# Two-layer trunk on one core: the feed-forward's first block with seven products for three chunk pairs, and other PSUM banks for the down blocks

## The chip, the core and the metric

The kernel runs on one core of one Trainium2 chip. The metric is the device time of one execution, in microseconds (us); the figure for a kernel is the median of its runs. The core has five engines with instruction queues of their own, which meet through semaphores: TensorE (matrix products, shown as PE, its weight loads as PEld), VectorE (DVE), ScalarE (ACT), GpSimd (POOL) and SyncE (SP, which here issues the loads of weights). Matrix products accumulate in eight PSUM banks of 128 x 512 float32 each, numbered 0 to 7.

## What is computed

Two layers over 256 tokens of width 2048, in float32. Each layer is a mixer (layer 0: sparse attention and gated linear attention; layer 1: stick-breaking attention), a feed-forward and a gated embedding, each with a normalisation ahead and a residual behind. The change lies in the feed-forward:

```python
def _swiglu(h, norm_g, w_gate, w_up, w_down):
    xn = _rmsnorm(h, norm_g)
    return (jax.nn.silu(xn @ w_gate) * (xn @ w_up)) @ w_down

for i in range(DEPTH):                      # DEPTH = 2
    h = h + mixer_i(h)
    h = h + _swiglu(h, ffn_norm[i], ffn_w_gate[i], ffn_w_up[i], ffn_w_down[i])
    gate = jax.nn.sigmoid(_rmsnorm(h, ple_norm[i]) @ ple_w_gate[i])
    h = h + (p[i] @ ple_w_proj[i]) * gate
```

The hidden width is 5632, which makes 11 blocks of 512 columns in each feed-forward.

## The kernel before

**Precision.** Every float32 operand of a product is split in two parts: ScalarE casts the high part (line 106) and VectorE subtracts it from the value to get the low part (line 107). A product is then three matmuls: high by high, high by low, low by high. Activations are split once; weights are split as they stream in.

**Units and tiles.** A `unit` loads four chunks of 128 weight rows (1 MB, one DMA of SP) into a raw tile; there are three raw tiles in turn inside the feed-forward. It splits two chunks at a time into a pair of tiles `whi` and `wlo`, of which there are four in turn, and with each pair of tiles issues 12 matmuls: two chunks by two halves of 128 tokens by three. A `block` is the units over all chunks of one set of 512 columns; its two banks (one for each half of the tokens) come in turn from banks 0 and 1 or 2 and 3 (`mm_tile`), unless the caller names them. Work that belongs to other steps, such as the turns of the next operand (`turn_h`), waits in a queue (`later`) and is taken out one entry for each pair of chunks (`tick`), or at once where it is needed (`need`). The order on each engine is not that of the source: a scheduler places an instruction earlier where its operands are ready earlier.

**The feed-forward.** The 11 blocks go in groups of three, three, three and two. For each block, gate and up columns are computed, then silu(gate) times up is turned across partitions (`cross`, line 143 and DMAs) and split into the hidden operand (`split_hid`). While the blocks of a group are computed, the four down blocks of the group before are placed behind them: one behind each of the first two blocks of a group, two behind the third, or two behind each block of the last group. A down block adds its two banks to the residual h (`add_to_h`, line 268). The down blocks of the last group come at the end.

**Seven products.** Blocks 1 to 10 (`gate_up_7`) do the first 6 of the 16 chunks in three chunk pairs. For a chunk pair, two halves of the tokens, gate and up, the plain way has 8 products; here there are 7, of sums of the operands. The sums of the operand (`sums_of_operand`, lines 837 to 845, into `ST`) are made once in a feed-forward; the sums of the weights (lines 858, 861, 862, into `T`) for each pair. A pair is four pieces of 6, 6, 6 and 3 matmuls (line 849), with banks as below. The other 10 chunks are classical units: after each of the first two pairs one of gate, after the third pair the last half unit of gate and then all of up. The combinations of the banks are put together by a ScalarE copy and VectorE adds into `E` (lines 898 to 907). Block 0 (`gate_up_8`) is two classical blocks; its products go straight to silu and to the product with up.

```python
    B2, B4, B3, B22, B1, B5, B6, B7 = range(8)
            pieces = [(None, raw[:, :, 0], [(B1, tok(0, 0)), (B2, tok(1, 0))]),
                      (sums_13, T[:, 0:2], [(B5, comb(0)), (B7, comb(2))]),
                      (sums_24, T[:, 2:4], [(B6, comb(1)), (B4, tok(1, 1))]),
                      (None, raw[:, 1, 1:2], [(B3, comb(3))])]
```

So bank 0 is B2, bank 1 is B4, bank 2 is B3, bank 3 is B22, bank 4 is B1, and banks 5, 6 and 7 are B5, B6 and B7.

Of the kernel before, what the change touches and what calls it, by code (L numbers as in the profile page):

```python
# [9 lines left out]
F32 = mybir.dt.float32  # L10
F32R = mybir.dt.float32r
I32 = mybir.dt.int32
AF = mybir.ActivationFunctionType
# [3 lines left out]
P = 128  # L17
NT = 2
# [9 lines left out]
def trunk_kernel(ctx: ExitStack, tc: tile.TileContext, x, p, even_norm, even_w_in, even_w_gk,  # L28
# [179 lines left out]

    def unit(ps, stat, k0, cols, first, last, nk=KU, kw0=None, step=KU, pre=None, begun=0):

# [11 lines left out]
        for j in range(0, nk, 2):  # L222
# [5 lines left out]
            for c in range(2):  # L228
                k = k0 + j + c
                for tt in range(NT):  # L230
                    sh = stat[0][:, k, tt * P:(tt + 1) * P]
                    sl = stat[1][:, k, tt * P:(tt + 1) * P]
                    st = first and tt >= begun and j + c == 0
                    en = last and j + c == nk - 1
                    nc.tensor.matmul(ps[tt][:, :n], sh, hi[:, c, :n], start=st, stop=False)  # L235
                    nc.tensor.matmul(ps[tt][:, :n], sh, lo[:, c, :n], start=False, stop=False)  # L236
                    nc.tensor.matmul(ps[tt][:, :n], sl, hi[:, c, :n], start=False, stop=en)  # L237
# [589 lines left out]
    def ffn(i, xs, nkey, nx_fn, fp):  # L827
# [22 lines left out]

        def pair(j, b):

# [21 lines left out]
            for n, (made, src, ps) in enumerate(pieces):  # L874
# [5 lines left out]
                for c, (p, stat) in enumerate(ps):  # L880
                    product(p, stat, hi[:, c], lo[:, c], j == 0, j == NS - 1 and p >= B1)
                if n % 2:
                    tick()

        def gate_up_7(b):
            need(("sT", i))
            rest = [(n, k) for n in range(2) for k in range(2 * NS, KC, KU)]

            def classical(n, k):
                nk = min(KU, KC - k)  # L890
                unit([bank[:, 2 * n], bank[:, 2 * n + 1]], xs, k, [((ffn_w_gate[i], ffn_w_up[i])[n], b * NB, NB)],
                     n == 1 and k == 2 * NS, k + nk == KC, nk=nk, begun=1)

            for j in range(NS):
                pair(j, b)
                if j < NS - 1:
                    classical(*rest.pop(0))
# [16 lines left out]

        def gate_up_8(b):
            pg = block(xs, [(ffn_w_gate[i], b * NB, NB)], key=nkey)
            rs = rstd_of(nkey)
            sl = fp.tile([P, NT, NB], F32, name="sl", bufs=1)
            for tt in range(NT):
                nc.scalar.activation(sl[:, tt], pg[tt], AF.Silu, scale=rs[:, tt:tt + 1])  # L920
            later(sums_of_operand, key=("sT", i))
            return sl, block(xs, [(ffn_w_up[i], b * NB, NB)])

        def split_hid(dst, x, k0):
# [4 lines left out]

        def gate_up(gi, n):  # L930
            b = groups[gi][n]
            if n == 0:
                hT[gi] = (fp.tile([P, 12, NT * P], F32R, name="hH"), fp.tile([P, 12, NT * P], F32R, name="hL"))
            sl, pu = gate_up_7(b) if b else gate_up_8(b)
            rs = rstd_of(nkey)
# [6 lines left out]

        def down(gi, cb, nx):
            for b in groups[gi]:
                need(("hT", i, b))
            nk = 4 * len(groups[gi])
            ps = block(hT[gi], [(ffn_w_down[i], cb * NB, NB)], nk=nk, kw=groups[gi][0] * 4)
            add_to_h(ps, cb)
            if nx:
                finish_cols(nx, cb)  # L950

        third["pool"] = fp
        for gi, g in enumerate(groups):
            for n in range(len(g)):
                gate_up(gi, n)
                if gi:
                    for cb in range(4 * n // len(g), 4 * (n + 1) // len(g)):
                        down(gi - 1, cb, None)
        nx = nx_fn()
# [161 lines left out]
```

## Time and profile before

| | us |
|---|---|
| median of 3 runs | 2417.17 (2416.87 to 2420.09) |
| the profiled execution | 2414.99 |
| its span, first to last instruction | 2413.3 |
| TensorE busy in it | 2385.1 |
| VectorE busy in it | 1722.3 |
| ScalarE busy in it | 1269.2 |

The span is what the profile shows of an execution; the difference to the execution's own time lies before and after it. The mean granted clock of TensorE is 0.999 of full speed. Times in the rows are from the span's start. A matmul's time overlaps that of its neighbours, so the cost of one is read from start to start. "idle before" is the time that an engine stood still ahead of an instruction, with what ended it; a group of instructions is named by line, engine, operation and output<-input tile. The feed-forward of layer 0 begins at about 388.9 us, that of layer 1 at about 1591.5 us.

### The profile page before, as it was taken

The numbers are of one execution on the slowest core, as the hardware profiler recorded it, in microseconds if no ns is written. First come the engines' busy times: TensorE is split into PE (matmuls) and PEld (weight loads), VectorE is DVE, ScalarE is ACT, GpSimd is POOL, SyncE is SP. The second block draws the span as 40 slices with busy tenths as digits, with TensorE's granted clock in tenths as the row PEclk, the third lists the DMA queues.
The fourth block names the chain that finished last, engine by engine and source line by source line (L and its number), as shares of the span: only waits on it lengthen the run. The fifth ranks groups of instructions, "written<-read, shape, count | busy, mean of one in ns | idle before, by whom it ended". The sixth has DMA issues, their size and how long they took to land.

```text
span 2413.3 us, 28118 instructions
## 1 busy us (share of the span) xinstructions
PE 2385.1 (99%) x10786; PEld 1959.9 (81%) x10786; DVE 1722.3 (71%) x2009; ACT 1269.2 (53%) x1560; POOL 105.3 (4%) x177
## 2 busy tenths in 40 slices
PE   8999999999999999999999999999999999999998
PEld 7887788788888888888888888887888888888887
DVE  5765456898878877855666666568988778777564
ACT  6644445555545545546546655555655455445463
POOL 0000100010000000000000000000000000000000
PEclk9999999999999999999999999999999999999999
DMA  6454455566666666555554454556666666666563
GB/s 213 141 178 140 157 207 182 194 228 215 218 221 210 212 224 226 196 197 183 175 192 157 157 178 166 203 186 199 234 213 214 212 210 212 221 231 204 178 235 122
DMA packets 240681, 473.13 MB, mean 196 GB/s; under 512 B 12849, under 2 KB 19729, under 8 KB 240418
## 3 DMA queue, kind: packets, MB, share of 16 engines
q1 hardware_dynamic: 232514, 447.07, 55.8%
q0 software_dynamic: 7744, 23.08, 3.1%
q8 instruction: 84, 1.38, 0.2%
q10 hardware_dynamic: 288, 1.18, 0.1%
q14 instruction: 51, 0.42, 0.0%
HBM read 457.66 MB, written 13.63 MB: 195 GB/s over the span
## 4 chain that ended last, share of the span: by engine, by line
PE 79%; DVE 9%; DMA 6%; ACT 3%; issue 2%; SPq 0%; DVEq 0%; ACTq 0%; POOLq 0%; POOL 0%
PE bank L236 22%; PE bank L237 22%; PE bank L235 22%; PE bank L849 9%; DVE wlo L107 4%; DMA raw<-in_ffn_w_up_dram 3%; DMA raw<-in_odd_w_in_dram 2%; DVE kT L135 1%; ACT whi L106 1%; PE bank L165 1%; DVE work L858 1%; DVE work L907 1%; DVE tq L143 0%; DVE sl L937 0%; DMA raw<-in_even_w_in_dram 0%
## 5 line engine op out<-in xcount | busy, mean ns | idle before, releaser
L107 DVE TENSOR_TENSOR wlo<-raw,whi 128x1024 fp32r<-128x1024 f32 (+2 forms) x848 | 982.8, 1172 | 474.6 <-ACT whi L106 470.3
L106 ACT CAST whi<-raw 128x1024 fp32r<-128x1024 f32 (+2 forms) x848 | 851.6, 1011 | 839.6 <-PE bank L237 561.7
L236 PE MATMUL bank<-wlo,aH 128*128 128x512 f32 (+2 forms) x2176 | 844.4, 388 | 6.8 <-DVE wlo L107 6.0
L235 PE MATMUL bank<-whi,aH 128*128 128x512 f32 (+2 forms) x2176 | 849.3, 391 | 0.6 <-ACT whi L106 0.6
L237 PE MATMUL bank<-whi,aL 128*128 128x512 f32 (+2 forms) x2176 | 842.4, 387 | 0.0
L236 PEld LDWEIGHTS bank<-wlo,aH 128*128 128x128 f32 x2176 | 409.3, 188 | 96.2 <-DVE wlo L107 16.2
L235 PEld LDWEIGHTS bank<-whi,aH 128*128 128x128 f32 x2176 | 409.1, 188 | 84.2 <-issue 2.8
L237 PEld LDWEIGHTS bank<-whi,aL 128*128 128x128 f32 x2176 | 409.0, 188 | 83.9 <-issue 1.0
L235 PE MATMUL bank<-whi,hH 128*128 128x512 f32 x704 | 277.2, 394 | 0.0
L236 PE MATMUL bank<-wlo,hH 128*128 128x512 f32 x704 | 277.0, 393 | 0.0
L237 PE MATMUL bank<-whi,hL 128*128 128x512 f32 x704 | 273.6, 389 | 0.0
L106 ACT CAST whi<-work 128x1024 fp32r<-128x1024 f32 x120 | 126.0, 1050 | 159.6 <-PE bank L237 81.9
L107 DVE TENSOR_TENSOR wlo<-work,whi 128x1024 fp32r<-128x1024 f32 x120 | 146.6, 1222 | 57.1 <-ACT whi L106 56.3
L849 PE MATMUL bank<-whi,sT 128*128 128x512 f32 x480 | 167.4, 389 | 0.0
L235 PEld LDWEIGHTS bank<-whi,hH 128*128 128x128 f32 x704 | 132.2, 188 | 30.0
L237 PEld LDWEIGHTS bank<-whi,hL 128*128 128x128 f32 x704 | 132.1, 188 | 29.7
L236 PEld LDWEIGHTS bank<-wlo,hH 128*128 128x128 f32 x704 | 132.4, 188 | 26.1
L849 PEld LDWEIGHTS bank<-whi,sT 128*128 128x128 f32 x480 | 90.1, 188 | 18.6
L147 POOL DMA_DIRECT2D ty<-tq x88 | 48.5, 560 | 1095.5 <-DVE tq L143 987.3
L849 PE MATMUL bank<-wlo,sT 128*128 128x512 f32 x240 | 94.0, 392 | 0.5 <-DVE wlo L107 0.4
L858 DVE TENSOR_TENSOR work<-raw 128x1024 f32<-128x1024 f32 x60 | 73.4, 1223 | 25.5 <-DMA raw<-in_ffn_w_up_dram 25.1
L849 PE MATMUL bank<-whi,aH 128*128 128x512 f32 x180 | 70.7, 393 | 4.3 <-DVE h L268 4.3
(253 smaller groups left out, 1620.0 us busy)
## 6 DMA issues: line engine op xcount, KB each, us to landing
raw<-in_ffn_w_down_dram SPq DMA_DIRECT2D x88, 1024.0 KB, 5.2
raw<-in_ffn_w_gate_dram SPq DMA_DIRECT2D x48, 1024.0 KB, 5.2
raw<-in_ffn_w_up_dram SPq DMA_DIRECT2D x48, 1024.0 KB, 5.2
raw<-in_odd_w_in_dram SPq DMA_DIRECT2D x48, 1024.0 KB, 5.2
raw<-in_ffn_w_gate_dram SPq DMA_DIRECT2D x80, 512.0 KB, 3.9
raw<-in_ffn_w_up_dram SPq DMA_DIRECT2D x80, 512.0 KB, 4.8
raw<-in_even_w_in_dram SPq DMA_DIRECT2D x36, 1024.0 KB, 5.0
raw<-in_ple_w_gate_dram SPq DMA_DIRECT2D x28, 1024.0 KB, 5.1
```

Source lines behind the costliest of these rows:

```text
L106: state["cast"] = nc.scalar.copy(hi, raw).ins
L107: nc.vector.tensor_tensor(lo, raw, hi.bitcast(F32), OP.subtract)
L135: nc.vector.transpose(dst[32 * a:32 * a + 32, :, :, 32 * q:32 * q + 32], src.rearrange("p t (m a c) -> p t m a c", a=4, c=32)[32 * q:32 * ...
L147: nc.gpsimd.dma_start(y[:, :, q].rearrange("a c t n -> c a (t n)"), tq[32 * q:32 * q + 32].rearrange("c a t m r -> c a (t m r)"))
L165: nc.tensor.transpose(ps[:, c, tt, :], h[:, tt, k * P:(k + 1) * P], ident)
L235: nc.tensor.matmul(ps[tt][:, :n], sh, hi[:, c, :n], start=st, stop=False)
L236: nc.tensor.matmul(ps[tt][:, :n], sh, lo[:, c, :n], start=False, stop=False)
L237: nc.tensor.matmul(ps[tt][:, :n], sl, hi[:, c, :n], start=False, stop=en)
L849: nc.tensor.matmul(bank[:, p], a, b, start=first and m == 0, stop=last and m == 2)
L858: nc.vector.tensor_tensor(T[:, 0:2], raw[:, 0], raw[:, :, 1], OP.add)
L907: nc.vector.tensor_tensor(e, bank[:, 2 * n:2 * n + 2], e, OP.add)
```

## The change

Block 0 of each feed-forward now goes the same way as the others, with one difference in order. Two classical units (chunks 6 to 9 of gate, then of up) come first; then all turns of the operand and its sums are asked for; then come the three pairs with a classical unit after each of the first two (chunks 10 to 13 of gate, then of up), and last the half units (chunks 14 and 15) of gate and of up. A set `begun` notes which banks have been started. `gate_up_8` is gone. The queue entry for `sums_of_operand` is made ahead of the two units and may be taken at once. The down blocks that stand between blocks get their banks by name: the last one behind a block banks 1 and 6 (B4, B6), one before it banks 0 and 5 (B2, B5). The last group's down blocks take turns on banks 0 to 3 as before.

```diff
--- before.py
+++ after.py
@@ -206,7 +206,7 @@
             return third["pool"].tile([P, KU, NB], F32, name="raw3", bufs=1)
         return wp.tile([P, KU, NB], F32, name="raw", bufs=2)
 
-    def unit(ps, stat, k0, cols, first, last, nk=KU, kw0=None, step=KU, pre=None, begun=0):
+    def unit(ps, stat, k0, cols, first, last, nk=KU, kw0=None, step=KU, pre=None, starts=None):
 
 
         kw0 = k0 if kw0 is None else kw0
@@ -230,7 +230,7 @@
                 for tt in range(NT):
                     sh = stat[0][:, k, tt * P:(tt + 1) * P]
                     sl = stat[1][:, k, tt * P:(tt + 1) * P]
-                    st = first and tt >= begun and j + c == 0
+                    st = (first if starts is None else starts[tt]) and j + c == 0
                     en = last and j + c == nk - 1
                     nc.tensor.matmul(ps[tt][:, :n], sh, hi[:, c, :n], start=st, stop=False)
                     nc.tensor.matmul(ps[tt][:, :n], sh, lo[:, c, :n], start=False, stop=False)
@@ -848,7 +848,7 @@
             for m, (a, b) in enumerate(((stat[0], hi), (stat[0], lo), (stat[1], hi))):
                 nc.tensor.matmul(bank[:, p], a, b, start=first and m == 0, stop=last and m == 2)
 
-        def pair(j, b):
+        def pair(j, b, begun):
 
             raw = raw_tile().rearrange("p (r c) n -> p r c n", r=2)
             for c, w in enumerate((ffn_w_gate[i], ffn_w_up[i])):
@@ -878,21 +878,35 @@
                 lo = wp.tile([P, 2, NB], F32R, name="wlo")
                 split_sb(src, hi[:, :len(ps)], lo[:, :len(ps)])
                 for c, (p, stat) in enumerate(ps):
-                    product(p, stat, hi[:, c], lo[:, c], j == 0, j == NS - 1 and p >= B1)
+                    product(p, stat, hi[:, c], lo[:, c], p not in begun, j == NS - 1 and p >= B1)
+                    begun.add(p)
                 if n % 2:
                     tick()
 
-        def gate_up_7(b):
-            need(("sT", i))
+        def gate_up(b):
+            begun = set()
             rest = [(n, k) for n in range(2) for k in range(2 * NS, KC, KU)]
 
             def classical(n, k):
                 nk = min(KU, KC - k)
-                unit([bank[:, 2 * n], bank[:, 2 * n + 1]], xs, k, [((ffn_w_gate[i], ffn_w_up[i])[n], b * NB, NB)],
-                     n == 1 and k == 2 * NS, k + nk == KC, nk=nk, begun=1)
-
+                ps = (2 * n, 2 * n + 1)
+                for c in range(k // 2, (k + nk) // 2):
+                    need((nkey, c))
+                unit([bank[:, p] for p in ps], xs, k, [((ffn_w_gate[i], ffn_w_up[i])[n], b * NB, NB)],
+                     False, k + nk == KC, nk=nk, starts=[p not in begun for p in ps])
+                begun.update(ps)
+
+            if b == 0:
+
+                later(sums_of_operand, key=("sT", i), delay=0)
+                rest.sort(key=lambda u: u[1])
+                classical(*rest.pop(0))
+                classical(*rest.pop(0))
+                for c in range(KC // 2):
+                    need((nkey, c))
+                need(("sT", i))
             for j in range(NS):
-                pair(j, b)
+                pair(j, b, begun)
                 if j < NS - 1:
                     classical(*rest.pop(0))
             nc.scalar.copy(E[:, 0], bank[:, B1])
@@ -912,26 +926,17 @@
             turns["mm"] = 0
             return sl, [E[:, 2 + tt] for tt in range(NT)]
 
-        def gate_up_8(b):
-            pg = block(xs, [(ffn_w_gate[i], b * NB, NB)], key=nkey)
-            rs = rstd_of(nkey)
-            sl = fp.tile([P, NT, NB], F32, name="sl", bufs=1)
-            for tt in range(NT):
-                nc.scalar.activation(sl[:, tt], pg[tt], AF.Silu, scale=rs[:, tt:tt + 1])
-            later(sums_of_operand, key=("sT", i))
-            return sl, block(xs, [(ffn_w_up[i], b * NB, NB)])
-
         def split_hid(dst, x, k0):
             d = [dst[n][:, k0:k0 + 4, :].rearrange("p m (q r) -> p m q r", q=8) for n in range(2)]
             with tc.issue_after(state["cast"]):
                 nc.scalar.copy(d[0], x)
             nc.vector.tensor_tensor(d[1], x, d[0].bitcast(F32), OP.subtract)
 
-        def gate_up(gi, n):
+        def hidden(gi, n):
             b = groups[gi][n]
             if n == 0:
                 hT[gi] = (fp.tile([P, 12, NT * P], F32R, name="hH"), fp.tile([P, 12, NT * P], F32R, name="hL"))
-            sl, pu = gate_up_7(b) if b else gate_up_8(b)
+            sl, pu = gate_up(b)
             rs = rstd_of(nkey)
             for tt in range(NT):
                 nc.vector.scalar_tensor_tensor(sl[:, tt], pu[tt], rs[:, tt:tt + 1], sl[:, tt], op0=OP.mult,
@@ -940,11 +945,11 @@
             later(lambda: x.update(x=cross(sl, fp)), key=("xT", i, b))
             later(lambda: split_hid(hT[gi], x["x"], 4 * n), key=("hT", i, b), after=(("xT", i, b), 10))
 
-        def down(gi, cb, nx):
+        def down(gi, cb, nx, ps=None):
             for b in groups[gi]:
                 need(("hT", i, b))
             nk = 4 * len(groups[gi])
-            ps = block(hT[gi], [(ffn_w_down[i], cb * NB, NB)], nk=nk, kw=groups[gi][0] * 4)
+            ps = block(hT[gi], [(ffn_w_down[i], cb * NB, NB)], nk=nk, kw=groups[gi][0] * 4, ps=ps)
             add_to_h(ps, cb)
             if nx:
                 finish_cols(nx, cb)
@@ -952,10 +957,13 @@
         third["pool"] = fp
         for gi, g in enumerate(groups):
             for n in range(len(g)):
-                gate_up(gi, n)
+                hidden(gi, n)
                 if gi:
-                    for cb in range(4 * n // len(g), 4 * (n + 1) // len(g)):
-                        down(gi - 1, cb, None)
+                    cbs = range(4 * n // len(g), 4 * (n + 1) // len(g))
+                    for cb in cbs:
+
+                        ps = (B4, B6) if cb == cbs[-1] else (B2, B5)
+                        down(gi - 1, cb, None, [bank[:, p] for p in ps])
         nx = nx_fn()
         for cb in range(4):
             down(len(groups) - 1, cb, nx)
```

## Rows read from the trace of the kernel before

**Rows 1.** The page's first part: each engine's busy time, share and instructions.

```profile
PE 2385.1 (99%) x10786; PEld 1959.9 (81%) x10786; DVE 1722.3 (71%) x2009; ACT 1269.2 (53%) x1560; POOL 105.3 (4%) x177
```

**Rows 2.** Stretches of blocks 0 and 2: length, then PE, PEld, DVE, ACT, POOL busy.

```profile
388.90:433.30 44.40, 44.40 (x201) 36.77 (x200) 31.02 (x35) 22.41 (x27) 3.01 (x1) 1.00 0.56 180
...
476.70:518.90 42.20, 42.09 (x183) 33.87 (x182) 39.67 (x42) 24.24 (x26) 3.69 (x6) 1.00 0.69 226
```

**Rows 3.** Waits of TensorE, feed-forward 0, then 1: us, times, longest.

```profile
PE bank L849 <- DVE h L268: 1.8, 3, 0.9
PE bank L236 <- DVE wlo L107: 0.8, 1, 0.8
...
PE bank L849 <- DVE h L268: 2.5, 3, 1.1
PE bank L236 <- DVE wlo L107: 1.2, 2, 0.8
```

**Rows 4.** Line 235 on TensorE from 402 to 419 us: durations, first and last start.

```profile
L235 PE MATMUL bank<-whi,aH x25: 389/389/389, 402.1 to 418.4; 128*128 128x512 f32 x25
```

**Rows 5.** Timeline of TensorE: transposes, two bank waits, a pair's start (start, us, ...).

```profile
394.30 0.60 PE L165 MATMUL bank<-ident,h 128*128 128x128 f32 x4
...
771.22 0.50 PE L849 MATMUL bank<-whi,aH 128*128 128x512 f32 x1 [0.39 <-DVE h L268]
...
828.97 0.39 PE L849 MATMUL bank<-whi,aH 128*128 128x512 f32 x1
...
1840.35 0.50 PE L849 MATMUL bank<-whi,aH 128*128 128x512 f32 x1 [1.12 <-DVE h L268]
```

**Rows 6.** Timeline of VectorE after the pair's start at 828.97 us.

```profile
829.98 1.28 DVE L268 TENSOR_TENSOR h<-bank,h 128x512 f32<-128x512 f32 x2
...
833.10 1.22 DVE L107 TENSOR_TENSOR wlo<-raw,whi 128x1024 fp32r<-128x1024 f32 x1
```

**Rows 7.** Timeline of VectorE at the start of layer 0's feed-forward.

```profile
388.61 1.28 DVE L268 TENSOR_TENSOR h<-bank,h 128x512 f32<-128x512 f32 x2
389.81 1.75 DVE L837 TENSOR_TENSOR work<-aH,aL 128x1536 f32<-128x1536 f32 x1
...
399.86 1.22 DVE L107 TENSOR_TENSOR wlo<-raw,whi 128x1024 fp32r<-128x1024 f32 x1
400.99 0.48 DVE L171 SCALAR_TENSOR_TENSOR aL<-bank,gT,aH 128x256 fp32r<-128x256 f32 x1
```

**Rows 8.** Timeline of SP's queue and ScalarE: block 2's first pair is loaded, cast.

```profile
466.35 0.37 SPq L855 DMA_DIRECT2D raw<-in_ffn_w_gate_dram  x1
...
470.49 1.05 ACT L106 CAST whi<-raw 128x1024 fp32r<-128x1024 f32 x1 [2.99 <-DMA raw<-in_ffn_w_gate_dram]
```

**Rows 9.** Timeline of VectorE, handover from block 1 to block 2.

```profile
471.57 1.23 DVE L107 TENSOR_TENSOR wlo<-raw,whi 128x1024 fp32r<-128x1024 f32 x1 [1.84 <-ACT whi L106]
472.71 1.22 DVE L858 TENSOR_TENSOR work<-raw 128x1024 f32<-128x1024 f32 x1
...
475.30 2.50 DVE L107 TENSOR_TENSOR wlo<-work,whi 128x1024 fp32r<-128x1024 f32 x2
477.72 1.22 DVE L907 TENSOR_TENSOR work<-bank,work 128x1024 f32<-128x1024 f32 x1
...
479.45 1.41 DVE L937 SCALAR_TENSOR_TENSOR sl<-work,rstd,sl 128x512 f32<-128x512 f32 x2
```

**Rows 10.** Groups of VectorE by shape in block 1: busy us, mean ns, idle before.

```profile
L143 DVE STREAM_TRANSPOSE tq<-sl 128x1024 f32<-128x1024 f32 x1 | 1.2, 1239 | 0.0
...
L899 DVE TENSOR_TENSOR work<-bank,work 128x512 f32<-128x512 f32 x1 | 0.7, 683 | 0.0
```

**Rows 11.** Timeline of VectorE and TensorE in block 1, second pair.

```profile
446.55 1.22 DVE L858 TENSOR_TENSOR work<-raw 128x1024 f32<-128x1024 f32 x1 [2.08 <-DMA raw<-in_ffn_w_up_dram]
...
448.43 0.50 PE L849 MATMUL bank<-wlo,sT 128*128 128x512 f32 x1 [0.42 <-DVE wlo L107]
...
450.17 0.50 PE L236 MATMUL bank<-wlo,aH 128*128 128x512 f32 x1 [0.78 <-DVE wlo L107]
```

## The prediction

> **What bounds the kernel now.** I read the engine line of the page first: TensorE is busy for 99% of the span, VectorE (DVE) for 71% and ScalarE for less [rows 1]. So time is won by giving TensorE fewer matmuls or fewer waits. But the 71% is a mean over unlike stages, so next I cut the start of the first feed-forward into its blocks [rows 2]. Block 0, the only one done classically, keeps DVE busy for 31.0 of 44.4 us. Block 2, with seven products for each chunk pair, keeps it busy for 39.7 of 42.2 us, 94%, and TensorE still hardly waits. The change turns the first kind of block into the second and leaves DVE its other duties there, so DVE is the engine to watch.
>
> The waits come next [rows 3]. In both feed-forwards TensorE lost 4.3 us (1.8 and 2.5, six times) before products of L849 because the residual add of L268 had not yet emptied a bank, and about 2 us because a low part (wlo) was late.
>
> **Matmuls removed (-4.1).** A classical pair takes 8 products, the other form 7, each of 3 matmuls; three pairs give 9 matmuls a block, two blocks 18. In a stretch without waits, 25 starts of L235, one in every three matmuls, lie between 402.1 and 418.4 [rows 4]: 16.3/24/3 = 0.226 us for each. 18 x 0.226 = 4.1 us. The 389 ns of one matmul overlaps its neighbours and isn't the price. [...]
>
> **Other banks for the down blocks (-4.0).** With one down block behind a block, its sums sit in banks 0 and 1, and the next block's second product (B2, bank 0) must wait for the add. In the new code the last down block has banks 1 and 6, which the pair reaches only after 15 and 12 matmuls (3.4 and 2.7 us); the adds are done 2.3 us after the pair's start in one of the later cases (828.97 to 829.98 + 1.28) [rows 5, 6]. So the 4.3 us go, plus 0.11 us for each stretched matmul behind a wait (0.50 against 0.39), 5.0 in all: the upper bound. Some comes back, because DVE goes from add to split without a pause: the following unit's first low part is ready at 833.10 + 1.22 = 834.3, and TensorE, freed, would want it at 828.97 + 22 x 0.226 = 833.9 [rows 5, 6]. That is 0.4 us lost where the wait was long, perhaps 1.0 over all six. I take 4.0, bounds 2.5 and 5.0.
>
> **A bank wait added (+0.6).** In layer 0 the mixer's last output block ends in banks 0 and 1 (fourteen blocks take turns on two bank pairs before it), and the first classical unit now starts in just these; before, the gate block took banks 2 and 3. In layer 1 the turn falls the other way and nothing waits. The price is the nearest rows', the same add before a product: 0.39 to 1.12 us [rows 5]; DVE has no queue ahead of this add, it goes straight from one to the next (388.61, then 389.81) [rows 7], so 0.6. Behind the last group of down blocks a similar meeting (bank 1) is covered by three matmuls, 0.68 us, about as long as an add; I cost it at nothing, 0.3 if DVE is late.
>
> **Moved: sums of the operand and the last turns.** These were already executed right behind the mixer (from L837 at 389.81 to the last turn at 400.99 + 0.48 = 401.5) [rows 7], so their place hardly changes, but their cover does. The pair now reaches TensorE at about 388.9 + 0.6 + 48 x 0.226 + 0.9 for eight transposes (four take 0.60, in part under the matmul before [rows 5]) = 401.2. Until 401.5 DVE did four splits beside these duties, the last at 399.86; two of the four now wait for the chunk sums (L858, L861, L862, some 2.4 us), so the third piece's low part is there at about 404, where TensorE wants it at 404.1. Cost 0.4 us a layer, bounds 0 and 1.0.
>
> **Handover from block 0 to block 1: the large unknown.** Count from the start of block 0's third pair on TensorE. It ends at 4.75 us; two units of 12 matmuls follow, ending at 7.5 and 10.2; then block 1's first pair begins, and the second matmul on its third piece needs a low part at 13.1. In the other blocks 48 more matmuls lie between. The pair's weights go into the buffer that pair three used; its last split comes 1.7 us in (tile buffer free at 0, cast 0.6, split 0.7, signals 0.4). Gate weights land 4.1 us after issue (466.35 to 470.49) [rows 8], so at 5.8. From there, in the handover from block 1 to block 2, cast, split, three sums and two splits end at 477.8, 7.3 us after the landing [rows 8, 9]; here that is 13.1. Exactly on time, if DVE does nothing else. But it has the four E sums (0.7 us each [rows 10]; first possible at 3.7, when B6 and the copy of B1 are there; with one split they last until about 7.3, and the first piece's high part is there at 6.9: 0.4 late), and the add on banks 0 and 1 (L907; 1.15, the pitch of [rows 9]): 1.5 us late at the least. If the second L907 also goes first, 2.6; the two L937 too, 4.0; the transpose L143 too, 5.2 [rows 10]. In [rows 9] L907 came behind the third piece and L937 behind that; here DVE is later, so I expect L907 in front and L937 behind: 2.6. With the 0.4 of the start, 3.0 a layer, 6.0 in all; bounds 2 x 1.5 = 3.0 and 2 x (5.2 + 1.0) = 12.4. ScalarE gets one copy of a bank more, under the casts' pauses; 0.6 us if they are gone.
>
> **Sum.** -4.1 - 4.0 + 0.6 + 6.0 = -1.5 us. The profiled execution took 2414.99 us, a span of 2413.3 and 1.7 around it; it would take 2413.5. The median of the three runs is 2417.17, 2.2 above it; I predict 2415.7 for the median. With every bound at its end: -5.6, or +7.0.
>
> **Rivals.**
> B, the cover holds (faster). The handover costs only its least, and block 1's present waits disappear: there a sum blocked DVE for 2.08 us until weights landed, and TensorE waited 0.42 and 0.78, in layer 1 0.8 [rows 3, 11]. A TensorE that arrives later finds them landed: -4.1 - 4.0 + 0.6 + 3.0 - 2.0 = -6.5, 2410.7. For it speaks that both are one slack counted twice; against it, that the late pair also delays the next loads.
> C, DVE becomes the bound (slower). At the handover it works in the order of the code, both L907, L937 and the transpose before the splits: the upper ends, +7, 2424. It decides from 12 us for both layers, six a layer. For it: in [rows 11] TensorE waited behind a sum that DVE had taken early, with the needed split queued behind. [...] Against it: [rows 9], where the order was better.
> D, the banks bring nothing: the six waits pass to the next low part. -4.1 + 0.6 + 6.0 = +2.5, 2419.7. Against it: only 0.4 us of lateness in [rows 6].
>
> **How the numbers follow.** 0.2%, 4.8 us, is about what a measurement of this kernel can tell from no change. My forecast (A), all but 1.5 us given back: 0.55, of which 0.03 spills over into faster and 0.01 into slower. B 0.23, C 0.13, D 0.09 (no change). Faster 0.26, same 0.51 + 0.09 = 0.60, slower 0.14. The range 2410 to 2423 reaches almost to B's and C's times; some 0.09 of B and 0.08 of C lie outside.
>
> **What would show it.** 18 fewer matmuls. No wait of L849 on L268 in the down blocks; a wait of the first L235 of layer 0's feed-forward on L268 of 0.4 to 1.1 us. In blocks 0 and 1 TensorE waits for wlo of L107 at block 1's first pair, 1.5 to 5 us, the second and third piece, with L907 ahead of them on DVE. I am wrong if these waits stay under 1.5 us a layer, or pass 6; or if blocks 3 to 10 change by more than their bank waits.

## The result, and the profile after

The changed kernel takes 2431.17 us (median of 5 runs, 2428.96 to 2434.78) against 2417.85 of the kernel before (5 runs): a ratio of 1.0054, 95% interval 1.0043 to 1.0065. It is 13.3 us slower, where I forecast 1.5 us faster and put the worst of all bounds at 7.0 us slower.

The first line of the page and the window of block 0 (length; busy PE, PEld, DVE, ACT, POOL; granted clock; DMA share; GB/s) show the part that went as planned. Line numbers above 862 move with the change: L907 is now L921, L928 is L933, L937 is L942.

```profile
PE 2392.7 (98%) x10768; PEld 1959.5 (81%) x10768; DVE 1754.1 (72%) x2051; ACT 1277.4 (53%) x1574; POOL 102.1 (4%) x177
```

```profile
389.80:433.60 43.80, 43.37 (x192) 34.88 (x191) 40.75 (x49) 24.07 (x31) 1.12 (x1) 1.00 0.48 160
```

TensorE has 18 matmuls fewer than in [rows 1]. Block 0 has become what block 2 was in [rows 2]: DVE is busy for 40.75 of 43.8 us (31.02 of 44.40 before), and inside the block TensorE still hardly waits, 0.43 us. The loss lies behind it. The same waits as in [rows 3], feed-forward 0 and then 1:

```profile
PE bank L236 <- DVE wlo L107: 7.4, 7, 2.8
PE bank L849 <- DVE wlo L107: 2.7, 3, 2.2
PE bank L849 <- ACT whi L106: 0.8, 2, 0.6
...
PE bank L236 <- DVE wlo L107: 3.9, 7, 0.8
PE bank L849 <- ACT whi L106: 2.3, 3, 1.8
PE bank L849 <- DVE wlo L107: 1.2, 2, 0.9
```

The line L849 from L268 is gone. In its place stand 18.3 us of waits for split weights, where before all waits in the two feed-forwards come to 6.7, the 6.3 of [rows 3] and the 0.42 of L849 in [rows 11]. Of the 18.3, 6.1 lie at the two handovers from block 0 to block 1, 0.9 at the two starts, 3.9 in the rest of blocks 1 and 2 (2.0 before) and 7.4 in blocks 3 to 10 (4.8 before). Now the handover and what follows it in layer 0, first as a timeline of TensorE (start, duration, ..., idle before and what ended it).

```profile
435.74 0.73 PE L849 MATMUL bank<-whi,sT 128*128 128x512 f32 x2 [0.56 <-ACT whi L106]
438.68 0.79 PE L849 MATMUL bank<-wlo,sT 128*128 128x512 f32 x1 [2.21 <-DVE wlo L107]
...
442.68 0.49 PE L849 MATMUL bank<-wlo,sT 128*128 128x512 f32 x1 [0.27 <-DVE wlo L107]
...
457.52 0.50 PE L236 MATMUL bank<-wlo,aH 128*128 128x512 f32 x1 [2.80 <-DVE wlo L107]
...
459.53 0.63 PE L237 MATMUL bank<-whi,aL 128*128 128x512 f32 x1
459.96 0.63 PE L235 MATMUL bank<-whi,aH 128*128 128x512 f32 x1
460.38 0.63 PE L236 MATMUL bank<-wlo,aH 128*128 128x512 f32 x1
```

The first three are the handover: block 1's first pair starts at 433.65 and waits for its second piece (435.74, 438.68) and its third (442.68). The fourth is new: it stands in the unit behind block 1's second pair. The last three lines show something else: nothing waits there, and yet the starts are 0.43 us apart instead of 0.226. The windows with the granted clock (the column behind the five busy times) say why, in both layers:

```profile
434.80:438.70 3.90, 1.13 (x5) 0.32 (x3) 3.90 (x6) 0.88 (x1) 0.00 (x0) 0.96 0.36 140
438.70:442.10 3.40, 3.40 (x8) 2.15 (x8) 3.40 (x4) 2.77 (x4) 0.99 (x2) 0.54 0.02 5
...
455.00:458.80 3.80, 1.28 (x6) 1.07 (x7) 3.70 (x4) 1.04 (x1) 0.00 (x0) 1.00 0.08 30
458.80:462.20 3.40, 3.40 (x10) 2.63 (x9) 3.36 (x4) 0.00 (x0) 0.00 (x0) 0.51 0.69 219
1648.00:1653.70 5.70, 2.93 (x12) 1.73 (x11) 5.70 (x8) 3.31 (x5) 0.00 (x0) 0.99 0.39 148
1653.70:1660.50 6.80, 6.53 (x15) 4.05 (x14) 6.43 (x7) 4.80 (x6) 2.22 (x4) 0.51 0.53 121
```

Three times TensorE stood still for much of a stretch (busy for 1.13 of 3.90, 1.28 of 3.80 and 2.93 of 5.70 us), and each time the next 3.4 or 6.8 us ran at a clock of 0.51 to 0.54. The starts in one of these stretches are 0.42 to 0.43 us apart (459.53, 459.96, 460.38), 1.9 times the 0.226 at full clock.

On DVE, the handover looks like this:

```profile
432.08 1.22 DVE L921 TENSOR_TENSOR work<-bank,work 128x1024 f32<-128x1024 f32 x1
433.21 1.22 DVE L858 TENSOR_TENSOR work<-raw 128x1024 f32<-128x1024 f32 x1
434.34 1.22 DVE L921 TENSOR_TENSOR work<-bank,work 128x1024 f32<-128x1024 f32 x1
435.48 0.68 DVE L861 TENSOR_TENSOR work<-work,raw 128x512 f32<-128x512 f32 x1
436.08 1.41 DVE L942 SCALAR_TENSOR_TENSOR sl<-work,rstd,sl 128x512 f32<-128x512 f32 x2
437.40 1.22 DVE L107 TENSOR_TENSOR wlo<-work,whi 128x1024 fp32r<-128x1024 f32 x1
438.54 0.68 DVE L862 TENSOR_TENSOR work<-work,raw 128x512 f32<-128x512 f32 x1
439.14 1.24 DVE L143 STREAM_TRANSPOSE tq<-sl 128x1024 f32<-128x1024 f32 x1
440.30 1.18 DVE L858 TENSOR_TENSOR work<-raw 128x1024 f32<-128x1024 f32 x1
441.40 1.22 DVE L107 TENSOR_TENSOR wlo<-work,whi 128x1024 fp32r<-128x1024 f32 x1
...
455.10 1.23 DVE L858 TENSOR_TENSOR work<-raw 128x1024 f32<-128x1024 f32 x1 [3.00 <-DMA raw<-in_ffn_w_up_dram]
456.24 3.49 DVE L107 TENSOR_TENSOR wlo<-raw,whi 128x1024 fp32r<-128x1024 f32 x3
```

DVE never pauses here. It works off both L921, both L942, then the second piece's split (437.40); the transpose, a sum of the *next* pair (440.30), and only then the third piece's split (441.40). Further on it stands still for 3.00 us with a sum whose weights have not landed at its head, and does three splits as soon as that sum is out of the way.

The first wait of the handover is ended by ScalarE's cast, not by DVE: 0.56 us in layer 0, 1.84 in layer 1. In layer 1 the cast (1650.09) stands in ScalarE's queue behind an ACT_TABLE_LOAD of 1.28 us (1647.56, on the line of the silu) and the two silu themselves. There the waits after it are shorter by as much: 3.04 us of waits at the handover in both layers.

**The ledger.** Both profiled executions cut into two feed-forwards, before and then after; length less PE busy is TensorE's idle time.

```profile
380.00:1030.00 650.00, 646.67 (x2831) 529.17 (x2830) 519.17 (x530) 335.16 (x354) 42.38 (x65) 1.00 0.65 212
...
1580.00:2240.00 660.00, 655.82 (x2872) 536.76 (x2871) 524.05 (x535) 340.02 (x359) 43.62 (x67) 1.00 0.65 213
```

```profile
380.00:1045.00 665.00, 653.83 (x2840) 532.17 (x2839) 537.05 (x553) 340.97 (x363) 40.49 (x65) 0.99 0.64 209
...
1595.00:2260.00 665.00, 657.09 (x2854) 534.53 (x2853) 539.38 (x555) 342.82 (x364) 42.22 (x67) 0.99 0.64 211
```

The spans are 2413.3 and 2433.0, 19.7 us apart. Idle time grew from 3.3 + 4.2 to 11.2 + 7.9, by 11.6; of the 3.4 + 3.4 + 6.8 us at a clock of 0.51 to 0.54 an estimated half was lost, 6.8; the matmuls left out are -4.1. That is 14.3. Of the other 5.4, 1.8 lie ahead of the first feed-forward (1.0) and between the two (0.8); the remainder is matmuls that last 0.50 or 0.79 around waits, and what is not itemised. The profiled execution is the slowest of the five; the medians differ by 13.3. The five go with their mean clock: 2434.78 at 0.996, 2432.24 and 2431.17 at 0.997, 2429.22 and 2428.96 at 0.998.

### The profile page after: what moved, and what is told of

Same layout as the page of the kernel before. It is cut to its first block, busy times and chain, and to the rows that moved or that the text cites. A ratio compares the mean times of both kernels' runs of the same rounds, so it can differ in the third digit from the quotient of the medians.

```text
span 2433.0 us, 28171 instructions
## 1 busy us (share of the span) xinstructions
PE 2392.7 (98%) x10768; PEld 1959.5 (81%) x10768; DVE 1754.1 (72%) x2051; ACT 1277.4 (53%) x1574; POOL 102.1 (4%) x177
## 4 chain that ended last, share of the span: by engine, by line
PE 74%; DVE 13%; DMA 7%; ACT 3%; issue 3%; SPq 0%; DVEq 0%; ACTq 0%; POOLq 0%; POOL 0%
PE bank L236 21%; PE bank L237 21%; PE bank L235 21%; PE bank L849 7%; DVE wlo L107 6%; DMA raw<-in_ffn_w_up_dram 4%; DVE work L858 1%; DMA raw<-in_odd_w_in_dram 1%; DVE kT L135 1%; ACT whi L106 1%; DVE work L921 1%; PE bank L165 1%; DVE hL L933 1%; DVE work L861 1%; DVE sl L942 1%
## 5 line engine op out<-in xcount | busy, mean ns | idle before, releaser
L236 PE MATMUL bank<-wlo,aH 128*128 128x512 f32 (+2 forms) x2128 | 827.7, 389 | 16.0 <-DVE wlo L107 15.4
L235 PE MATMUL bank<-whi,aH 128*128 128x512 f32 (+2 forms) x2128 | 832.2, 392 | 1.3 <-ACT whi L106 1.3
L237 PE MATMUL bank<-whi,aL 128*128 128x512 f32 (+2 forms) x2128 | 824.5, 388 | 0.0
L236 PEld LDWEIGHTS bank<-wlo,aH 128*128 128x128 f32 x2128 | 400.8, 188 | 107.1 <-DVE wlo L107 29.1
L237 PEld LDWEIGHTS bank<-whi,aL 128*128 128x128 f32 x2128 | 400.6, 188 | 82.1 <-issue 1.0
L106 ACT CAST whi<-work 128x1024 fp32r<-128x1024 f32 x132 | 138.5, 1050 | 192.5 <-PE bank L237 80.2
L107 DVE TENSOR_TENSOR wlo<-work,whi 128x1024 fp32r<-128x1024 f32 x132 | 161.2, 1222 | 56.1 <-ACT whi L106 55.3
L849 PE MATMUL bank<-whi,sT 128*128 128x512 f32 x528 | 187.7, 395 | 3.1 <-ACT whi L106 3.1
L849 PEld LDWEIGHTS bank<-whi,sT 128*128 128x128 f32 x528 | 100.0, 190 | 27.0 <-ACT whi L106 7.0
L849 PE MATMUL bank<-wlo,sT 128*128 128x512 f32 x264 | 105.1, 398 | 4.1 <-DVE wlo L107 3.9
L858 DVE TENSOR_TENSOR work<-raw 128x1024 f32<-128x1024 f32 x66 | 80.6, 1221 | 35.2 <-DMA raw<-in_ffn_w_up_dram 34.8
L849 PE MATMUL bank<-whi,aH 128*128 128x512 f32 x198 | 77.6, 392 | 0.0
```

Of the source, the lines that this page charges most:

```text
L106: state["cast"] = nc.scalar.copy(hi, raw).ins
L107: nc.vector.tensor_tensor(lo, raw, hi.bitcast(F32), OP.subtract)
L849: nc.tensor.matmul(bank[:, p], a, b, start=first and m == 0, stop=last and m == 2)
L858: nc.vector.tensor_tensor(T[:, 0:2], raw[:, 0], raw[:, :, 1], OP.add)
```

## The experiments

Ratios are to the kernel before, run beside them (its median is 2417.39 for the first four, 2418.33 for the next four, 2417.48 for the last four).

| kernel | median us | ratio, 95% interval |
|---|---|---|
| banks only | 2416.93 | 0.9996 [0.9987, 1.0004] |
| block 0 only | 2432.21 | 1.0056 [1.0043, 1.0068] |
| half units early | 2421.22 | 1.0014 [1.0005, 1.0023] |
| product deferred | 2423.26 | 1.0018 [1.0009, 1.0027] |
| idle filled | 2430.11 | 1.0045 [1.0033, 1.0058] |
| half units early, product deferred | 2417.97 | 0.9995 [0.9986, 1.0004] |
| two pairs | 2420.21 | 1.0007 [0.9998, 1.0015] |
| two pairs, product deferred | 2416.49 | 0.9993 [0.9984, 1.0002] |
| two pairs, deferred in all blocks | 2412.55 | 0.9977 [0.9967, 0.9986] |
| before, deferred in blocks 1 to 10 | 2415.23 | 0.9986 [0.9977, 0.9995] |
| half units early, deferred in all blocks | 2414.46 | 0.9985 [0.9976, 0.9993] |
| sum behind the splits | 2427.87 | 1.0039 [1.0026, 1.0051] |

### Banks only: the kernel before, with the new banks of the down blocks

```diff
-        def down(gi, cb, nx):
+        def down(gi, cb, nx, ps=None):
...
-            ps = block(hT[gi], [(ffn_w_down[i], cb * NB, NB)], nk=nk, kw=groups[gi][0] * 4)
+            ps = block(hT[gi], [(ffn_w_down[i], cb * NB, NB)], nk=nk, kw=groups[gi][0] * 4, ps=ps)
...
-                    for cb in range(4 * n // len(g), 4 * (n + 1) // len(g)):
-                        down(gi - 1, cb, None)
+                    cbs = range(4 * n // len(g), 4 * (n + 1) // len(g))
+                    for cb in cbs:
+                        ps = (B4, B6) if cb == cbs[-1] else (B2, B5)
+                        down(gi - 1, cb, None, [bank[:, p] for p in ps])
```

> The kernel before with nothing changed but the banks of the down blocks. Theory 1 (the six bank waits pass on to the next low part, so the banks bring nothing; the loss is block 0's): no change, 2416 to 2420 us, no wait of L849 on the add of h, and new waits of about 0.5 to 1.5 us on wlo of L107 behind the down blocks. Theory 2 (the named banks do harm by themselves): 2421 to 2424. The prediction's step: 4.0 us faster, 2414.

The time is the same. TensorE's waits in feed-forward 0, then 1, and two waits from its timeline:

```profile
PE bank L236 <- DVE wlo L107: 2.3, 4, 0.7
...
PE bank L236 <- DVE wlo L107: 4.2, 8, 0.8
PE bank L849 <- DVE h L268: 0.2, 1, 0.2
```

```profile
785.75 0.50 PE L236 MATMUL bank<-wlo,aH 128*128 128x512 f32 x1 [0.61 <-DVE wlo L107]
...
844.98 0.50 PE L236 MATMUL bank<-wlo,aH 128*128 128x512 f32 x1 [0.66 <-DVE wlo L107]
```

DVE ahead of the first of them:

```profile
780.99 1.23 DVE L858 TENSOR_TENSOR work<-raw 128x1024 f32<-128x1024 f32 x1 [1.21 <-DMA raw<-in_ffn_w_up_dram]
```

Of the 4.3 us of bank waits 0.2 are left, and the waits for low parts have grown from 2.4 us (2.0 in [rows 3], 0.42 in [rows 11]) to 6.5: 6.7 in all, before and here. In [rows 5] TensorE waited at 771.22; here it passes that place and waits 14 us later, in the unit behind the pair, until DVE's low part is there. What sets that moment is DVE's queue: it stood still for 1.21 us with a sum at its head whose weights had not landed (780.99), and from there it worked without a pause until that low part was done. The bank only decided at which instruction TensorE met the delay. This is rival D.

### Block 0 only: the changed kernel, with the old banks of the down blocks

```diff
-                        down(gi - 1, cb, None, [bank[:, p] for p in ps])
+                        down(gi - 1, cb, None)
```

> The changed kernel with the down blocks on the banks of before. Theory 1 (all of the loss is block 0's): 2428 to 2433, as the changed kernel. Theory 2 (banks do harm): 3 us or more below the changed kernel, 2425 to 2428. The prediction's step for this alone: 2.5 us slower than before, 2420.

As slow as the changed kernel, with bank waits of 1.4 and 3.3 us still there, the handover's waits unchanged (0.56 and 2.20) and 2.11 us where the changed kernel has 2.80. So block 0 carries the whole loss.

### Half units early: more work for TensorE behind the third pair

Block 0 has ten chunks for classical units. Here the half units (two chunks each) come between the pairs and the two full units behind the third pair, 48 matmuls in place of 24, before block 1 begins.

```diff
...
+                rest = [(0, 14, False), (1, 14, False), (0, 10, True), (1, 10, True)]
...
```

> The changed kernel with the two half units of block 0 set between its pairs and the two full units (48 matmuls in place of 24) behind the third pair. Theory 1 (the handover is short of cover): TensorE's waits at block 1's first pair fall from 3.6 us a layer to under 1, its granted clock does not fall behind them, 2420 to 2424. Theory 3 (the loss lies in VectorE's work at the start of block 0 and in late weights of block 1): the waits move into block 0, where the pairs stand closer, 2428 or more.

10 us come back. The waits at the handover are 0.17 and 1.01 us (layer 1: 0.22 and 1.07), and the clock doesn't fall:

```profile
436.00:444.00 8.00, 6.81 (x28) 4.80 (x27) 8.00 (x9) 3.31 (x4) 2.32 (x4) 1.00 0.38 119
```

The price is a wait inside block 0, where the shorter units cover less: 0.49 us at 420.78, 0.65 in layer 1.

### Product deferred: the same work, another order on DVE

Block 0's two L942 and its transpose are handed to the list of deferred work. In the trace the transpose then comes behind the splits of block 1's first pair (442.94); the two L942 (L943 there) come behind the second piece's split in layer 0 (437.61), and on both sides of it in layer 1.

```diff
...
+            def times():
+                for tt in range(NT):
+                    nc.vector.scalar_tensor_tensor(sl[:, tt], pu[tt], rs[:, tt:tt + 1], sl[:, tt], ...)
+
+            if b:
+                times()
+            else:
+                later(times)
...
-            later(lambda: x.update(x=cross(sl, fp)), key=("xT", i, b))
+            later(lambda: x.update(x=cross(sl, fp)), key=("xT", i, b), delay=2 if b else 4)
```

> The changed kernel with block 0's product of gate and up (two L942) and its transpose (L143) put in the queue, to be issued behind block 1's first pair: 2.6 us of VectorE's work a layer that no longer stands ahead of the pair's splits. Theory 1 (VectorE works in the order of the code): the waits at the first pair fall from 3.6 to about 1.5 us a layer, the clock does not fall there, 2423 to 2427. Theory 3 (late weights): the waits stay, 2429 or more.

8 us come back for 2.6 us of DVE work that is only moved (1.41 and 1.24). The handover's waits shrink little in layer 0, from 3.0 to 2.3 us (0.56, 0.88, 0.56, 0.29), but the wait of 2.80 at 457.52 is gone: block 1's second pair is loaded from 443.05 on, 2.5 us sooner than in the changed kernel (445.52). The clock stays full in layer 0 (1.00 from 436 to 444); in layer 1, where 1.83 and 0.89 us of waits remain, it falls once (0.71 from 1642 to 1645, 0.64 from there to 1652). These two waits are ended by ScalarE's casts, which the edit leaves where they were. ScalarE in layer 1:

```profile
1638.97 1.28 ACT L925 ACT_TABLE_LOAD   x1 [2.95 <-DVE work L921]
1640.26 1.33 ACT L925 ACTIVATE sl<-work,rstd 128x512 f32<-128x512 f32 x2
1641.51 1.03 ACT L106 CAST whi<-work 128x1024 fp32r<-128x1024 f32 x1
```

The cast ends at 1642.54 and TensorE goes on at 1642.59.

### Idle filled: what does the clock cost by itself?

Ten useless matmuls go into bank 3, which block 1 does not yet use, ahead of the second piece of its first pair. They take an estimated 2.3 us (10 x 0.226), where TensorE would have waited.

```diff
+                if b == 1 and (j, n) == (0, 0):
+                    for _ in range(10):
+                        nc.tensor.matmul(bank[:, B22], xs[0][:, 0, :P], xs[0].rearrange("p k n -> p (k n)")[:, :NB],
+                                         start=True, stop=True)
```

> The changed kernel with ten matmuls of no use (2.3 us a layer) ahead of the second piece of block 1's first pair, into a bank that is free there; the results are as before. Theory 4 (the granted clock falls because TensorE stands still there): the fall right behind the first pair is gone in both layers, the ten run inside the wait that is there anyway, 2425 to 2428 us. Theory 5 (the clock falls for another reason, or more work makes it fall more): the falls stay and the ten are added, 2431 to 2436.

The clock did what was expected, the time didn't. Windows of the handover in both layers, then a wait of layer 1:

```profile
436.00:444.00 8.00, 6.72 (x26) 4.22 (x25) 8.00 (x10) 4.26 (x5) 2.40 (x4) 1.00 0.23 58
...
1650.00:1662.00 12.00, 11.05 (x45) 8.38 (x46) 10.69 (x12) 7.22 (x9) 3.73 (x6) 1.00 0.79 244
```

```profile
1667.21 0.50 PE L236 MATMUL bank<-wlo,aH 128*128 128x512 f32 x1 [2.71 <-DVE wlo L107]
```

With the idle time filled, the two falls behind the first pair are gone, with DVE and the loads as they were. So these two falls hung on TensorE's standing still. But the median moves by 1 us only (2430.11 against 2431.17, intervals of the ratios overlap): in layer 1 TensorE now arrives early at weights that aren't split, and waits 2.71 us where it waited 0.53. The two falls had lasted 3.4 and 6.8 us at 0.54 and 0.51, with half of that, 5.1 us, as an estimate of the loss, and I had expected 3 to 6 us back. That step fell: a slow TensorE cost next to nothing here, because what it waited for next came no sooner.

### Half units early and product deferred together

> The changed kernel with both edits: half units of block 0 early, and its two L942 and its L143 behind block 1's first pair. Theory 1 (handover short of cover, VectorE's order): under 0.5 us of waits a layer at the first pair, full clock, 2416 to 2419. Theory 3 (VectorE's start and late weights keep the rest): 2421 or more, as with the half units alone.

The edits are those of the two kernels above. Handover waits of 0.46 and 0.28 us (layer 1: 0.46 and 0.25), full clock (a mean of 0.999), and the time of the kernel before. Edits at the handover alone thus return the whole 13.3 us. The 4.1 us of saved matmuls are not seen either: 9.8 us of waits are left in the two feed-forwards outside the handover's.

### Two pairs: one pair less in block 0

Two chunk pairs instead of three, with a unit more behind them (72 matmuls in classical units after the last pair); 12 matmuls fewer than before, not 18.

```diff
+            ns = NS if b else 2
+            rest = [(n, k) for n in range(2) for k in range(2 * ns, KC, KU)]
...
                 classical(*rest.pop(0))
+                classical(*rest.pop(2))
...
+            for j in range(ns):
```

> The changed kernel with two chunk pairs in block 0 in place of three, and 60 matmuls behind the second pair's 12-matmul unit of gate (72 in all) as in the other blocks: 12 matmuls less than before the change in place of 18 (2.7 us), 6.5 us less work on VectorE a layer. Theory 1 (VectorE has no room for the third pair ahead of the handover): waits at block 1's first pair under 0.5 us, 2414 to 2418. Theory 6 (block 0 can't pay for any pair, its start costs as much as the matmuls save): 2418 to 2421.

No wait at block 1's first pair, as expected, but not the time: 2.81 us at 1657.62 in layer 1, with a fall of the clock behind it (0.76 from 1657 to 1664), and 1.67 at 654.24. Ahead of both DVE stood still with a sum at the head of its queue whose weights had not landed (2.89 us until 1655.21, 2.27 until 649.49), as at 455.10 in the changed kernel.

### Two pairs, product deferred

> Two pairs in block 0 and the product and transpose of block 0 deferred. Theory 1: within 1 us of the kernel with two pairs, since that handover has its cover already, 2414 to 2418. If the order on VectorE matters even there: 2 us or more below it.

I took the order to be worth nothing once the handover has cover. It is worth 3.7 us (2416.49 against 2420.21, the intervals of the two ratios just overlap): the 1.67 at 654 becomes 0.88, and in layer 1 the longest wait is 1.6.

### Deferral in every block: with two pairs, in the kernel before, with three pairs

If order matters where there is cover, it should matter in all blocks. The three kernels defer the product and the transpose in every block (in the kernel before, whose block 0 is classical, in blocks 1 to 10):

```diff
-            if b:
-                times()
-            else:
-                later(times)
+            later(times)
...
-            later(lambda: x.update(x=cross(sl, fp)), key=("xT", i, b), delay=2 if b else 4)
+            later(lambda: x.update(x=cross(sl, fp)), key=("xT", i, b), delay=4)
```

> Two pairs in block 0, and product and transpose deferred in every block. If the order at every handover still costs TensorE something: 2411 to 2415 us, clearly faster than both kernels. If VectorE's whole work is what binds the blocks with pairs, the waits just move: 2415 to 2419.

> The kernel before with product and transpose deferred in blocks 1 to 10, block 0 and banks as they were. If the order at the handovers costs something by itself: 2412 to 2416, by block 1's waits and part of the bank waits. If it doesn't: 2416 to 2419. Beside the two-pair kernel it tells what the pairs in block 0 are worth: theory 1 says 1 to 2 us, theory 6 nothing.

> Three pairs in block 0, half units early, product and transpose deferred in every block. Theory 1: within 1 us of the same with block 0 alone deferred (2418), since the other handovers have their cover; 2416 to 2419. If the order matters there too: 2412 to 2416.

The first beats both kernels, by 0.23% against the kernel before. Its DVE at the same handover:

```profile
435.82 1.22 DVE L921 TENSOR_TENSOR work<-bank,work 128x1024 f32<-128x1024 f32 x1
436.96 0.68 DVE L107 TENSOR_TENSOR wlo<-raw,whi 128x512 fp32r<-128x512 f32 x1
437.56 1.41 DVE L943 SCALAR_TENSOR_TENSOR sl<-work,rstd,sl 128x512 f32<-128x512 f32 x2
438.88 2.35 DVE L107 TENSOR_TENSOR wlo<-raw,whi 128x1024 fp32r<-128x1024 f32 x2
441.15 1.24 DVE L143 STREAM_TRANSPOSE tq<-sl 128x1024 f32<-128x1024 f32 x1
```

Splits and the block's own duties now take turns, and TensorE doesn't wait here. Deferral alone, without one matmul less, gives 2415.23, 2.2 us below the kernel before. Its trace doesn't show where they come from: the profiled execution is as long as that of before (2414.85 and 2414.99), and TensorE's waits in its feed-forwards are longer (9.3 us against 6.7, 7.0 of them for banks). By the medians the kernel with two pairs is 2.7 us faster than this one, which is also what 12 matmuls take (12 x 0.226), and that with three pairs 0.8, which these runs don't tell from nothing. But both also have the new banks, and with them 0 and 1.3 us of bank waits; no run shows what the matmuls alone bring.

### Sum behind the splits: what made the wait of 2.80 us?

The sum of block 1's second and third pair (L858) may only be queued behind the splits of the unit before.

```diff
-        nc.vector.tensor_tensor(lo, raw, hi.bitcast(F32), OP.subtract)
+        state["low"] = nc.vector.tensor_tensor(lo, raw, hi.bitcast(F32), OP.subtract).ins
...
+            low = state["low"]
             def sums_13():
+                if b == 1 and j:
+                    with tc.issue_after(low):
+                        nc.vector.tensor_tensor(T[:, 0:2], raw[:, 0], raw[:, :, 1], OP.add)
+                    return
```

> The changed kernel with one thing moved: the first weight sums (L858) of block 1's second and third pair are held behind the splits of the unit before them on VectorE. Theory 7 (the 2.8 us wait after block 1's second pair is the queue: splits that are ready stand behind a sum whose weights haven't landed): that wait falls under 0.7 us and so does the clock's fall behind it, 2425 to 2429 us. Theory 3 (the weights themselves are late): the wait moves on to the third pair with its size, 2430 to 2433.

DVE around the same time, where the sum is now L862, and the window behind it:

```profile
450.64 0.69 DVE L107 TENSOR_TENSOR wlo<-raw,whi 128x512 fp32r<-128x512 f32 x1
451.67 2.54 DVE L107 TENSOR_TENSOR wlo<-raw,whi 128x1024 fp32r<-128x1024 f32 x2 [0.34 <-ACT whi L106]
454.13 1.22 DVE L862 TENSOR_TENSOR work<-raw 128x1024 f32<-128x1024 f32 x1
```

```profile
455.00:459.00 4.00, 4.00 (x20) 3.30 (x19) 3.82 (x5) 1.12 (x2) 0.00 (x0) 1.00 0.81 249
459.00:462.40 3.40, 3.40 (x17) 2.82 (x16) 2.26 (x3) 3.19 (x5) 0.00 (x0) 1.00 0.13 48
```

The two splits go first, the wait at 457.52 is gone, and the clock stays full here. One thing moved besides: as the third piece's split comes sooner too (440.48, before 441.40), the second pair is loaded 0.9 us sooner (444.60 against 445.52), which is less than the 2.80. The median is 3.3 us lower, though the intervals of the two ratios just overlap; the handover's own waits (0.56 and 2.21, 1.84 and 0.93) are as they were. The wait of 2.80 was made by the order in DVE's queue, not by the late weights alone. No run holds the sums back in all blocks.

## Why the prediction was wrong

**Matmuls removed (-4.1).** Right in count, 18, and in the pitch wherever nothing waits (432.75 to 433.65 are four starts, 0.225 each). But the sum took them as won in full. With the loss at the handover taken away they are not seen (2417.97 against 2418.33), and no run shows their worth by itself.

**Other banks for the down blocks (-4.0).** This step failed. The waits on L268 did go, as written, and their gain is nothing: 2416.93 against 2417.39. I had checked one following low part against TensorE and allowed 0.4 us for a later wait; the runs showed all of it coming back, at the next low parts (6.7 us of waits with the old banks and with the new). The bound of 2.5 should have been 0, the price of rival D, which I gave 0.09.

**A bank wait added (+0.6).** It did not come. The first classical unit of layer 0 starts its banks late by 0.11 us at most (390.31, 0.50 for 0.39), with two matmuls (389.82, 390.05) set ahead of it out of the order of the code.

**The start (+0.4).** Right: waits of 0.20 and 0.24 us at 404.98 and 406.24, 0.47 in layer 1. Block 0 itself takes DVE without loss, as its window shows.

**The handover (2.6 a layer).** Right place and tiles, and in the main the right mechanism; DVE's order was wrong. I set L907 ahead of the pair's splits and L937 behind; both L942 went ahead of the second piece's split and the transpose ahead of the third's, with a sum of the next pair besides. That is rival C's order. Further on DVE stood still for 3.00 us, until 455.10, with a sum at the head of its queue, although the casts for the three splits behind it had ended at 452.24, 453.59 and 454.90. The weights landed 6.2 us after the third pair's start (423.45 to 429.68), where I had 5.8: the last cast and split took 0.62 and 0.69, as counted, but the split ended 2.25 in, not 1.7, and the landing came 3.95 after the issue at 425.73. The 0.4 for signals within the 1.7 was my estimate, which no run shows by itself; from the end of that split to the issue the trace has 0.03. By TensorE's starts (434.79 to 435.74, less a pitch, and so on) it lost 3.5 us in layer 0 and 3.7 in layer 1, of which the trace names 3.0 as waits: inside my bounds of 1.5 to 5.2. Had the rest of the sum held, this step alone would have missed by 2 us. For ScalarE I had counted one copy more and had left out its silu, which stands in the handover too, in layer 1 behind a table load of 1.28 us. With DVE as late as it was, this added nothing (3.04 us of waits in both layers); with the product deferred it is what is left in layer 1.

**What the sum did not hold.** The largest failure is here: I priced the handover as one wait of 2.6 us a layer with nothing behind it. From -1.5 to +13.3 is 14.8 us; 4.0 of them are the banks, 2.0 the handover itself, -0.6 the bank wait that did not come, and 9.4 lie behind the handover. Two terms are absent. The first: a pair that was late gave up its raw tile late, so the next weights were asked for late (445.52, against 443.05 with the product deferred), and a sum that needed them sat in DVE's queue ahead of splits that were ready. Before, this cost 2.08 us of DVE and 0.42 to 0.78 of TensorE [rows 11]; now 3.00 and 2.80. I had that row in hand and used it as a gain, in rival B ("a TensorE that arrives later finds them landed"), with only a half sentence on the loads that move back as well; they did, and it became a loss of 2 us more. The second: the clock. I priced every wait at its own length, and behind three of these waits 3.4 to 6.8 us ran at a clock of 0.51 to 0.54; what that costs by itself is open, since two of these falls gone returned 1 us. Further back too, TensorE's waits in blocks 3 to 10 grew from 4.8 to 7.4 us although the bank waits went; for those blocks I had called any change beyond their bank waits a sign of being wrong.

So rival C came closest, in its mechanism and its sign, but its +7.0 (+6.9 by the bounds as stated, as the other end is -5.7) lacked the same two terms. With 0 for the banks, 3.6 for each handover and no +0.6, my own sum would have read -4.1 + 2 x (0.4 + 3.6) = +3.9; the other 9.4 are the second wait, the clock, and waits further back, which the experiments returned together by more cover or a better order at one seam, but did not separate into terms that add up.

## What to carry to other kernels

An average of 71% busy said nothing about this seam (DVE busy for 3.90 of 3.90 us behind its start): where a change gives the second engine more work just where the first runs out of cover, follow that engine's queue in the order in which it is issued, and through the next loads too. Before saving matmuls, try the order: moving 2.6 us of DVE work back in its queue was worth 8 us in the changed kernel, and some 2 us by the medians in the kernel before with no matmul saved, though there its trace doesn't show where. The wait for a bank that a late engine emptied wasn't won here by another bank (6.7 us of waits with either); ask first whether that engine would be late at the next instruction as well.

## What I had not expected of the hardware

Waits of TensorE of 2.8 us in all (0.56 and 2.21; 2.80; 1.84 and 0.93) were followed, three times in the profiled execution, by 3.4 or 6.8 us at the lower clock (0.51 to 0.54), and the five runs of the changed kernel go with their mean clock (2434.78 us at 0.996, 2428.96 at 0.998). It isn't a matter of the wait's length alone: in the kernel with the idle time filled, the wait of 2.66 us at 456.62 in layer 0 was followed by a fall (0.72 from 459.0 to 462.4), and that of 2.71 at 1667.21 in layer 1 was not (1.00 from 1666 to 1675). What tells the two apart stays open. And a fall need not cost what it seems to: two of the three gone returned 1 us.
